# Two attentions of a hybrid mixer: matmul order, rotation, and where sigmoids and values stand

## The chip, the cores and the metric

The kernel runs on one core of a Trainium2 chip. The metric is the device time of one execution in microseconds (us), lower is better. In the profile, PE is the matrix engine (TensorE), PEld its weight loads, DVE the vector engine, ACT the scalar engine (activations, copies, casts), POOL is GpSimd, SP the engine whose queue issues the DMAs. SBUF is the core's working memory with 128 partitions, PSUM the eight accumulator banks that PE writes.

## The reference, cut to what matters

The program is three transformer layers on 512 tokens of 1024 features. The change touches the mixer of the first layer, which sees 16 extra tokens in front (528 in all). It has two attentions of eight heads over the same input:

```python
# first attention ("stick breaking"): q, k, v of 64 columns a head
z = (q @ k.T) * 64 ** -0.5
log_1m = where(strict, log_sigmoid(-z), 0); csum = cumsum(log_1m)
a = where(strict, exp(log_sigmoid(z) + csum[-1] - csum), 0);  y_sb = (a @ v) @ w_sb_o
# second attention ("latent"): q, k, v from normed latents c_q (384), c_kv (256)
s = (q_nope @ k_nope.T + rope(q_rope) @ rope(k_r).T) * 96 ** -0.5   # 64 + 32 columns a head
p = softmax(where(chunk mask, s, -1e30));                 y_mla = (p @ v) @ w_mla_o
# rope(x): x1, x2 = halves of 16 columns -> [x1*cos - x2*sin, x1*sin + x2*cos]; k_r is shared by all heads
g = sigmoid(gate_pre + b_gate)                                  # two gates of 1024 columns
out = (g_sb * y_sb + g_mla * y_mla) @ w_out
```

## The kernel before, in words

Activations lie transposed: 128 features on the partitions, tokens along the columns. Every projection is made in three passes for precision: weights and inputs are split into a rounded part and a remainder (hi, lo), and hi*hi, hi*lo and lo*hi are added in PSUM. A weight tile is loaded by a DMA on SP's queue (`wdma`, line 277), then cast by ACT (line 286) and its remainder made by DVE (line 287); two raw and three cast buffers are in turn. Attention scores, transposes and value products are in plain float32, and each of their matmuls is two PE instructions in the trace.

Instructions are written in program order, and a planner sorts each engine's queue: among instructions that it thinks ready it takes the one with the lowest place in program order. `high_priority(offset=n)` moves what is written under it n places ahead. On the chip each engine then runs its queue strictly in that order.

Both attentions go through four pairs of heads (c = 0 to 3), and in each through four blocks of 128 queries (b = 0 to 3), whose keys grow from 144 to 528. `start(c, b)` writes the scores (line 721, and the mask as a matmul, line 724) and the chain on ACT and DVE that makes probabilities of them. `attn_t` transposes the probabilities on PE (line 672; the 16 last keys in line 684) and copies them out of PSUM (line 677). `attn_v` multiplies them with the values (line 695). While a chain runs, PE is given filler: `self.todo` holds generators that write projection matmuls (`step_lin`, line 343), one matmul for each step, or two of half width where all 528 keys are projected, and `fill(n)` takes n steps. In the first attention the filler is the next pair's q and k and the 16 tiles of the gates, in the latent one the next pair's q and k and the eight tiles of y_sb @ w_sb_o (`wo`). The scores of block b + 1 are written before the transposes of block b. Transposes, value products and their copies are all under `high_priority(offset=100)`.

In the first attention the two heads of a pair lie on partitions 0 to 63 and 64 to 127, and their score matmuls use one half of PE's rows each. In the latent one each head has its own tiles of 96 rows: 64 rows without rotation, and 32 with it. The rotated queries are made from four weight tiles: for each group of four heads one with the rotated columns, one with the halves of these columns swapped. `turn` multiplies the first by the cosine and the second by the signed sine, and DVE adds the two into each head's q (in `qdone`). The rotated key rows `kr` are copied by ACT into each head's k, eight times. PSUM holds two double banks for scores (z), two banks for projections (l) and two for transposes and value products (a).

Before the latent attention all 16 tiles of the two gates (`gs`, `gm`) go through the sigmoid on ACT. Then come the first pair's projections, the latent values (line 910, five token blocks of six matmuls), and the loop over pairs. Its filler `wo` takes 2, 1, 2 and 3 tiles for the four pairs. After it the output stage makes y_mla @ w_mla_o (line 301), multiplies by gm, adds gs, splits the sum (lines 291, 292) and multiplies by w_out. ACT holds one set of function tables at a time: one for exponential and logarithm, one for the sigmoid, one for the square root.

## Time and profile before

| | us |
|---|---|
| median of 3 runs (2532.6 to 2533.84) | 2532.71 |
| the profiled execution | 2533.2 |
| its span | 2531.4 |
| PE busy over the span | 2496.9 (99%), 13334 matmuls |
| DVE busy | 1360.7 (54%) |
| ACT busy | 993.6 (39%) |
| first attention | about 481 to 681 |
| latent attention | about 681 to 797 |
| output stage up to w_out | about 797 to 815 |

Times in the rows count from the span's start. The span is what lies between the first and the last instruction of the profiled execution. A matmul's end is modelled, so two matmuls of the timeline overlap, and the distance from one start to the next tells what PE gave to each. An idle time in square brackets stands before the instruction, with the instruction that ended it.

### The profile page before, as it was taken

How to read it: one execution, taken by the hardware profiler on the slowest of the kernel's cores; microseconds unless marked ns; L12 is line 12 of the kernel's file. 1: busy time of each engine (PE TensorE's matmuls, PEld its weight loads, DVE VectorE, ACT ScalarE, POOL GpSimd, SP SyncE). 2: the span in 40 equal slices, each digit the busy share in tenths (PEclk: the TensorE clock that was granted, in tenths of full speed). 3: DMA queues.
4: the chain of work that ended last, by engine and by line, in shares of the span. 5: the costliest groups of instructions: out<-in, count | busy, mean ns of one | idle time of the engine just before them, and what ended most of it. 6: DMA issues, size and time to landing. Idle time of an engine off the chain costs nothing.

```text
span 2531.4 us, 33257 instructions
## 1 busy us (share of the span) xinstructions
PE 2496.9 (99%) x13334; PEld 2081.7 (82%) x13334; DVE 1360.7 (54%) x2197; ACT 993.6 (39%) x1601; POOL 162.3 (6%) x159
## 2 busy tenths in 40 slices
PE   8999999999999999999999999999999999999999
PEld 8999998777677788888777888888888668888887
DVE  5323347455566562434668765345465775535544
ACT  4222235344654442223564633223344563323332
POOL 1101010000001010101001011001000001101100
PEclk9999999999999999999999999999999999999999
DMA  4322234212212433333322332332333123333332
GB/s 140 92 92 85 92 95 132 81 54 67 59 43 64 161 116 92 97 100 98 115 89 90 118 107 91 93 109 92 93 114 101 42 76 133 94 98 100 96 89 100
DMA packets 78932, 240.49 MB, mean 95 GB/s; under 512 B 9332, under 2 KB 11636, under 8 KB 78520
## 3 DMA queue, kind: packets, MB, share of 16 engines
q1 hardware_dynamic: 78776, 238.35, 30.4%
q8 instruction: 105, 1.72, 0.3%
q14 instruction: 51, 0.42, 0.1%
HBM read 226.24 MB, written 8.92 MB: 93 GB/s over the span
## 4 chain that ended last, share of the span: by engine, by line
PE 91%; DVE 4%; ACT 3%; issue 1%; DMA 1%; POOL 0%; SPq 0%; ACTq 0%; DVEq 0%
PE l L301 71%; PE l L328 5%; PE l L343 5%; PE l L314 2%; PE z L721 1%; PE a L695 1%; PE a L672 1%; ACT e L236 1%; PE s L1414 1%; DVE wlo L287 1%; ACT whi L286 1%; PE a L408 1%; PE a L393 1%; DMA wraw<-in_hyo 1%; PE a L1442 1%
## 5 line engine op out<-in xcount | busy, mean ns | idle before, releaser
L286 ACT CAST whi<-wraw 128x1024 fp32r<-128x1024 f32 (+4 forms) x456 | 432.9, 950 | 1032.1 <-PE l L301 781.7
L301 PE MATMUL l<-xh,whi 128*128 128x512 f32 (+3 forms) x2156 | 707.9, 355 | 0.0
L301 PE MATMUL l<-xh,wlo 128*128 128x512 f32 (+3 forms) x2156 | 705.8, 354 | 0.0
L301 PE MATMUL l<-xl,whi 128*128 128x512 f32 (+3 forms) x2156 | 705.5, 354 | 0.0
L287 DVE TENSOR_TENSOR wlo<-wraw,whi 128x1024 fp32r<-128x1024 f32 (+4 forms) x456 | 500.2, 1098 | 274.9 <-ACT whi L286 268.8
L301 PEld LDWEIGHTS l<-xh,whi 128*128 128x128 f32 (+1 forms) x2156 | 382.1, 188 | 56.9 <-issue 1.4
L301 PEld LDWEIGHTS l<-xh,wlo 128*128 128x128 f32 (+1 forms) x2156 | 381.9, 188 | 56.6 <-issue 1.0
L301 PEld LDWEIGHTS l<-xl,whi 128*128 128x128 f32 (+1 forms) x2156 | 382.2, 187 | 56.2 <-issue 1.2
L301 PE MATMUL l<-chh,wlo 128*128 128x512 f32 x384 | 149.4, 389 | 0.0
L301 PE MATMUL l<-chl,whi 128*128 128x512 f32 x384 | 149.4, 389 | 0.0
L301 PE MATMUL l<-chh,whi 128*128 128x512 f32 x384 | 149.4, 389 | 0.0
L301 PE MATMUL l<-hh,wlo 128*128 128x256 f32 (+2 forms) x528 | 140.3, 320 | 0.0
L301 PE MATMUL l<-hl,whi 128*128 128x256 f32 (+2 forms) x528 | 140.2, 320 | 0.0
L301 PE MATMUL l<-hh,whi 128*128 128x256 f32 (+2 forms) x528 | 140.1, 319 | 0.0
L247 POOL TENSOR_TENSOR t<-g,xrs 128x528 f32<-128x528 f32 (+1 forms) x44 | 75.1, 1708 | 646.0 <-ACT g L236 646.0
L247 POOL TENSOR_TENSOR cc<-cc,xrs 128x512 f32<-128x512 f32 x48 | 62.8, 1308 | 834.1 <-ACT cc L236 830.3
L247 DVE TENSOR_TENSOR t<-l,t 128x256 f32<-128x256 f32 (+1 forms) x66 | 32.3, 516 | 143.9 <-PE l L301 138.9
L301 PEld LDWEIGHTS l<-hh,whi 128*128 128x128 f32 x528 | 88.4, 188 | 6.9
L301 PEld LDWEIGHTS l<-hl,whi 128*128 128x128 f32 x528 | 88.2, 188 | 6.9
L301 PEld LDWEIGHTS l<-hh,wlo 128*128 128x128 f32 x528 | 88.3, 188 | 6.8
L247 DVE TENSOR_TENSOR g<-l,xrs 128x256 f32<-128x256 f32 (+1 forms) x66 | 32.3, 516 | 114.3 <-PE l L301 112.6
L247 DVE TENSOR_TENSOR cz<-l,xrs 128x512 f32<-128x512 f32 x48 | 33.2, 692 | 109.6 <-PE l L301 105.3
(350 smaller groups left out, 3463.6 us busy)
## 6 DMA issues: line engine op xcount, KB each, us to landing
wraw<-in_up SPq DMA_DIRECT2D x96, 512.0 KB, 3.5
wraw<-in_dn SPq DMA_DIRECT2D x64, 384.0 KB, 3.2
wraw<-in_ffn_g SPq DMA_DIRECT2D x44, 512.0 KB, 3.5
wraw<-in_ffn_u SPq DMA_DIRECT2D x44, 512.0 KB, 3.4
wraw<-in_ffn_d SPq DMA_DIRECT2D x32, 448.0 KB, 3.3
wraw<-in_hy SPq DMA_DIRECT2D x20, 512.0 KB, 3.5
wraw<-in_ffn_d SPq DMA_DIRECT2D x16, 512.0 KB, 3.6
wraw<-in_gate SPq DMA_DIRECT2D x16, 512.0 KB, 3.5
```

What stands on the lines that cost most here:

```text
L236: i = nc.scalar.activation(out, in_, f, **kw)
L247: return (eng or self.nc.vector).tensor_tensor(out, a, b, op=op)
L286: nc.scalar.copy(hi, raw)
L287: nc.vector.tensor_tensor(lo, raw, hi, op=ALU.subtract)
L301: self.nc.tensor.matmul(ps, a[:, k * m:(k + 1) * m], b[:, k0 + k, c0:c1], start=first and k == 0 and pi == 0, stop=last and k == kc - 1 an ...
L314: self.nc.tensor.matmul(ps[:c1 - c0, :n], a[:, k, c0:c1], b[:, j * n:(j + 1) * n], start=k == 0 and pi == 0, stop=k == nk - 1 and pi == 2)
L328: self.nc.tensor.matmul(ps, a[:, k * P:(k + 1) * P], b[:, k0 + k, t0:t1], start=k == 0 and pi == 0, stop=k == kc - 1 and pi == 2)
L343: self.nc.tensor.matmul(ps, a[:, k * P:(k + 1) * P], b[:, k, t0:t1], start=k == 0 and pi == 0, stop=k == kc - 1 and pi == 2)
L393: nc.tensor.matmul(ps[:w, i * 64:(i + 1) * 64], acc[:, c:c + w], self.ones[:, :64], start=True, stop=True)
L408: nc.tensor.matmul(p[:, c - a:c - a + w], r[:w, i:i + 1].to_broadcast([w, P]), self.ident[:w, :w], start=True, stop=True)
L672: nc.tensor.transpose(pt[:, j * P:(j + 1) * P], probs[hh][:, i * P:(i + 1) * P], self.ident)
L695: nc.tensor.matmul(po[64 * hh:64 * hh + 64, :], vt[:, i, (2 * c + hh) * 64:(2 * c + hh + 1) * 64], where[(i, hh)], start=i == 0, stop=i == nb)
```

## The change

Six things are changed, all in the first layer's mixer.

- `step_lin` with two=True takes one PSUM bank, runs all matmuls of the first 256 keys, evicts them, and then does the same for the other 272. Before, both banks were taken and the matmuls of the two alternated.
- The matmuls of `attn_t`, `last_keys` and `attn_v` no longer stand under the raised priority; only the copies out of PSUM do.
- The latent rotation takes two weight tiles, one with the first halves of all eight heads' rotated columns and one with the second halves. `turn` makes both products of each with cosine and sine, then their difference and sum, once for all heads (`turned`). Two DMAs for each head's q bring its rows; q and k have 128 rows now, 64 of them for the rotation, of which k is zero in the rows that belong to the other head.
- The keys' rotated rows are brought once, by eight DMAs, into four lasting tiles (two for each head of a pair), whose upper halves POOL sets to zero first.
- The eight sigmoids of gs stand behind the first pair's latent projections; those of gm stand in the output stage, two tiles ahead of their use.
- The latent values are written behind the first scores in place of six filler steps. The first pair's copies of q and k go to DVE. `wo` takes two tiles for each pair, and the numbers of filler steps differ.

```diff
@@ prep, consts @@
-    r["uq"] = np.concatenate([_wt(nope), _wt(rope), _wt(_swap(rope, 16))], axis=0)
+    rope = rope.reshape(384, 8, 2, 16).transpose(0, 2, 1, 3).reshape(384, 256)
+    r["uq"] = np.concatenate([_wt(nope), _wt(rope)], axis=0)
...
+    r["rope8"] = np.ascontiguousarray(np.stack([np.tile(t[:, META:], (8, 1)) for t in (cos, sin)], axis=1).astype(np.float32))
@@ step_lin @@
-        segs, ev = self.banks2() if two else self.banks1(c0)
-        for k in range(kc):
-            for pi, (a, b) in enumerate(((hi, x[0]), (hi, x[1]), (lo, x[0]))):
-                for ps, t0, t1 in segs:
-                    self.nc.tensor.matmul(ps, a[:, k * P:(k + 1) * P], b[:, k, t0:t1],
...
-                yield
-        with self.tc.high_priority(offset=1000):
-            done(ev)
+        n = 0
+        for c0, c1 in ((0, CUT), (CUT, TM)) if two else ((c0, c0 + T),):
+            ps = self.bank()[:, :c1 - c0]
+            for k in range(kc):
+                for pi, (a, b) in enumerate(((hi, x[0]), (hi, x[1]), (lo, x[0]))):
+                    self.nc.tensor.matmul(ps, a[:, k * P:(k + 1) * P], b[:, k, c0:c1],
                                           start=k == 0 and pi == 0, stop=k == kc - 1 and pi == 2)
+                    n += 1
+                    if not two or n % 2 == 0:
+                        yield
+            with self.tc.high_priority(offset=1000):
+                done(ps, c0, c1)
@@ mixer @@
-        for g, b in ((gs, 0), (gm, KD)):
-            for m in range(KD):
-                self.act(g[:, m, :], g[:, m, :], AF.Sigmoid, bias=self.v("b_gate", b + m))
+        def sigmoid(g, m):
+            self.act(g[:, m, :], g[:, m, :], AF.Sigmoid, bias=self.v("b_gate", m + (KD if g is gm else 0)))
...
+        for m in range(2):
+            sigmoid(gm, m)
         for m in range(KD):
+            if m < KD - 2:
+                sigmoid(gm, m + 2)
             ps = self.lin1(d["wo"][m][:, 512:], ymla, 4)
@@ attn_t (attn_v and last_keys alike) @@
-        with self.tc.high_priority(offset=100):
-            for g0 in range(0, len(slots), 4):
...
+        for g0 in range(0, len(slots), 4):
...
+            with self.tc.high_priority(offset=100):
                 (nc.vector.tensor_copy if (g0 // 4) % 2 else nc.scalar.copy)(at[:, :n1], pt[:, :n1])
@@ latent @@
+        ks = [[L.tile([P, TM], F32, name=f"k{hh}{i}") for i in range(2)] for hh in range(2)]
+        for i in range(2):
+            for hh in range(2):
+                k = ks[hh][i]
+                nc.gpsimd.memset(k[64:, :], 0.0)
+                for s_ in range(2):
+                    p = 64 + 32 * s_ + 16 * hh
+                    nc.sync.dma_start(k[p:p + 16, :], kr[16 * s_:16 * s_ + 16, :])
+        turned = L.tile([P, 2, T], F32, name="turned")
...
+                    def done(ps, a, b):
+                        self.tt(turned[:, j, :], ps, rope[:, 0, :], mul)
+                        self.tt(t[:, 1 - j, :], ps, rope[:, 1, :], mul)
+                        if j:
+                            self.tt(turned[:, 0, :], turned[:, 0, :], t[:, 0, :], ALU.subtract)
+                            self.tt(turned[:, 1, :], turned[:, 1, :], t[:, 1, :], add)
...
-                    q = L.tile([96, T], F32, name=f"q{hh}", bufs=2)
-                    self.copy(q[:64], ev[0][0][64 * hh:64 * hh + 64])
-                    i = 2 * (c % 2) + hh
-                    self.tt(q[64:96], t12[32 * i:32 * i + 32, 0, :], t12[32 * i:32 * i + 32, 1, :], add)
+            copy = nc.vector.tensor_copy if c == 0 else self.copy
+                    q = L.tile([P, T], F32, name=f"q{hh}", bufs=2)
+                    copy(q[:64], ps[64 * hh:64 * hh + 64])
+                    for s_ in range(2):
+                        nc.sync.dma_start(q[64 + 32 * s_:96 + 32 * s_, :], turned[32 * c:32 * c + 32, s_, :])
...
-                    for p, s in ev:
-                        self.copy(s(k[:64]), p[64 * hh:64 * hh + 64])
-                    self.copy(k[64:96], kr)
+                    copy(ks[hh][c % 2][:64, a:b], ps[64 * hh:64 * hh + 64])
...
+        sigmoids()
         for c in range(4):
-            nm = (2, 1, 2, 3)[c]
+            nm = 2
...
-            self.fill(6)
+            if c == 0:
+                values()
+            else:
+                self.fill(4)
             for b in range(4):
                 if b < 3:
                     nxt = start(c, b + 1)
-                    self.fill(5)
+                    self.fill(5 if b else 4)
                 t = self.attn_t(L, probs, c, b + 1, vt, ymla, b, rest[b % 2])
-                self.fill(4)
+                self.fill((3, 4, 4, 3)[b])
                 if b < 3:
                     self.attn_v(*t)
-                    self.fill(3 if b == 2 else 1)
+                    self.fill(5 if b == 2 else 1)
```

## Rows read from the trace of the kernel before

**Rows 1.** Table of stretches: engine, busy us (instructions); PEclk granted clock; DMA share, GB/s.
```profile
481.00:681.00 200.00, 193.68 (x1119) 144.38 (x1118) 112.16 (x179) 91.02 (x163) 3.39 (x31) 1.00 0.19 59
681.00:700.00 19.00, 16.39 (x76) 12.33 (x76) 8.23 (x15) 16.98 (x32) 0.00 (x0) 1.00 0.29 84
700.00:797.00 97.00, 94.87 (x641) 70.56 (x641) 64.04 (x176) 51.37 (x138) 0.00 (x0) 1.00 0.14 42
797.00:815.00 18.00, 18.00 (x79) 14.59 (x79) 8.83 (x15) 5.62 (x10) 8.34 (x5) 1.00 0.30 87
```

**Rows 2.** Timeline, PE: start us, us, engine, line, operation, out<-in, shapes [idle before <-releaser].
```profile
681.75 0.40 PE L343 MATMUL l<-cqh,whi 128*128 128x512 f32 x1
...
687.66 0.39 PE L343 MATMUL l<-cqh,wlo 128*128 128x512 f32 x1
```

**Rows 3.** Timeline, head of the latent attention, DVE, ACT and PE.
```profile
684.65 0.69 DVE L247 TENSOR_TENSOR t<-l,rope 128x512 f32<-128x512 f32 x1
...
684.85 3.18 ACT L236 ACTIVATE gm<-gm,vecs 128x512 f32<-128x512 f32 x5
...
689.90 1.18 ACT L243 COPY q<-l 64x512 f32<-64x512 f32 x2
...
691.13 0.40 PE L343 MATMUL l<-ckvh,whi 128*128 128x272 f32 x1 [2.37 <-ACT q L243]
...
699.70 0.65 PE L721 MATMUL z<-k,q 96*128 96x144 f32 x4
```

**Rows 4.** Table of PE's waits, first attention: us in total, times, longest.
```profile
PE a L672 <- ACT e L236: 3.9, 9, 0.7
PE l L343 <- DVE sbk L247: 2.1, 4, 0.6
```

**Rows 5.** Table of PE's waits, latent attention.
```profile
PE l L343 <- ACT q L243: 3.1, 2, 2.4
```

**Rows 6.** Chain of work that ended last, first attention: start us, us, what.
```profile
507.33 0.87 PE z L721 x2
...
520.26 0.64 PE z L721 x2
...
521.49 0.65 PE z L721 x4
...
561.04 0.64 PE z L721 x2
```

**Rows 7.** Timeline, PE, behind a value product of the latent attention.
```profile
743.14 0.50 PE L343 MATMUL l<-ysbl,whi 128*128 128x512 f32 x1
743.48 0.40 PE L343 MATMUL l<-ysbh,wlo 128*128 128x512 f32 x1
```

**Rows 8.** Timeline, PE, last transposes of the latent attention.
```profile
791.13 0.44 PE L672 MATMUL a<-cst,e 128*128 128x128 f32 x2 [1.09 <-DVE e L894]
```

**Rows 9.** Timeline, ACT, table load behind the first attention's last exponential.
```profile
673.64 1.28 ACT L232 ACT_TABLE_LOAD   x1
...
674.93 0.59 ACT L677 COPY at<-a 128x512 f32<-128x512 f32 x1
```

**Rows 10.** DMA issues: count, KB each, median us from issue to landing.
```profile
qt<-ra SPq DMA_DIRECT2D x32, 64.0 KB, 2.0
```

**Rows 11.** Timeline, PE, latent scores and transposes.
```profile
712.70 1.50 PE L721 MATMUL z<-k,q 96*128 96x264 f32 x6
714.04 0.71 PE L672 MATMUL a<-cst,e 128*128 128x128 f32 x5
714.58 0.38 PE L684 MATMUL a<-cst,e 128*16 128x128 f32 x2
```

**Rows 12.** Timeline, PE, last block of the second head pair, latent attention.
```profile
740.78 0.22 PE L724 MATMUL z<-masks,idb 128*128 128x128 bf16 x1
...
745.55 0.27 PE L672 MATMUL a<-cst,e 128*128 128x128 f32 x1
```

More of the change, by code (lines that the diff above doesn't have):

```diff
@@ L638, in mixer @@
             if True:
-                self.latent(st, cq, ckv, kr, masks[:, P:], ymla, ysb, gs)
+                self.latent(st, cq, ckv, kr, masks[:, P:], ymla, ysb, gs, lambda: [sigmoid(gs, m) for m in range(KD)])
         stP.close()
@@ L823, in stick, with latent @@
         self.attn_v(*late)
-    def latent(self, st, cq, ckv, kr, mask, ymla, ysb, gs):
+    def latent(self, st, cq, ckv, kr, mask, ymla, ysb, gs, sigmoids):
         nc, d = self.nc, self.d
@@ L828, in latent @@
         L = self.pool(st, "L")
-        rope = L.tile([P, 2, TM], F32, name="rope")
-        nc.sync.dma_start(rope, d["rope"])
+        rope = L.tile([P, 2, T], F32, name="rope")
+        nc.sync.dma_start(rope, d["rope8"])
         scale = float(96 ** -0.5)
@@ L834, in latent @@
         nc.gpsimd.memset(vt[:, 4, :], 0.0)
-        t12 = L.tile([P, 2, T], F32, name="t12")
+        ks = [[L.tile([P, TM], F32, name=f"k{hh}{i}") for i in range(2)] for hh in range(2)]
+        for i in range(2):
+            for hh in range(2):
+                k = ks[hh][i]
[4 more added lines that the diff above has]
+        turned = L.tile([P, 2, T], F32, name="turned")
@@ L836, in latent, with turn, done @@
         qk = {}
         def proj(c):
-            def turn(j):
-                def done(ev):
-                    self.tt(t12[:, j, :], ev[0][0], rope[:, j, META:], mul)
-                return done
-            if c % 2 == 0:
+            if c == 0:
+                t = L.tile([P, 2, T], F32, name="t12")
+                def turn(j):
+                    def done(ps, a, b):
+                        self.tt(turned[:, j, :], ps, rope[:, 0, :], mul)
[3 more added lines that the diff above has]
+                            self.tt(turned[:, 1, :], turned[:, 1, :], t[:, 1, :], add)
+                    return done
@@ L866, in wo, with done @@
         def wo(m):
-            def done(ev):
-                self.tt(gs[:, m, :], ev[0][0], gs[:, m, :], mul)
+            def done(ps, a, b):
+                self.tt(gs[:, m, :], ps, gs[:, m, :], mul)
             yield from self.step_lin(d["wo"][m][:, :512], ysb, 4, done)
@@ L903, in latent, with values @@
         self.fill()
-        w = self.wload(d["uv"][0], 1024)
-        for i in range(5):
-            a, b = i * P, min((i + 1) * P, TM)
-            ps = self.bank()[:b - a]
-            for k in range(2):
-                for pi, (xx, ww) in enumerate(((0, 0), (1, 0), (0, 1))):
-                    nc.tensor.matmul(ps, ckv[xx][:, k, a:b], w[ww][:, k * 512:(k + 1) * 512],
-                                     start=k == 0 and pi == 0, stop=k == 1 and pi == 2)
-            self.copy(vt[:b - a, i, :], ps)
+        def values():
+            w = self.wload(d["uv"][0], 1024)
+            for i in range(5):
+                a, b = i * P, min((i + 1) * P, TM)
+                ps = self.bank()[:b - a]
+                for k in range(2):
+                    for pi, (xx, ww) in enumerate(((0, 0), (1, 0), (0, 1))):
+                        nc.tensor.matmul(ps, ckv[xx][:, k, a:b], w[ww][:, k * 512:(k + 1) * 512],
+                                         start=k == 0 and pi == 0, stop=k == 1 and pi == 2)
+                self.copy(vt[:b - a, i, :], ps)
+        sigmoids()
         late, m = None, 0
         for c in range(4):
-            nm = (2, 1, 2, 3)[c]
+            nm = 2
             self.todo = ([proj(c + 1)] if c < 3 else []) + [wo(m + i) for i in range(nm)]
```

63 lines of the change are left out of this document (30 added, 33 removed).

## The prediction

> **What bounds the kernel now.** I read the page's busy shares first: TensorE (PE) is busy almost all the time, no other engine much above half. Then the table of stretches: the granted clock is 1.00 in all of them, PE stays 2 to 6 us short of full in each stretch of the attentions, and VectorE (DVE) and ScalarE (ACT) are busy for about half of each, DVE for two thirds in the latent one [rows 1]. Only at the head of the latent attention does ACT lead, with 16.98 of 19.00 us. So the time is the sum of what PE executes, of what it loses in changing between kinds of matmul, and of its waits. A step of the change is worth what it takes from that sum; work that leaves ACT or DVE counts only through a wait of PE, for which I read the table of waits and then the timeline around each. The profiled execution took 2533.2 us, its span is 2531.4, the median of the runs 2532.71; the sum below is made on the first, and 0.5 us comes off for the median.
>
> **The parts and their costs.**
>
> *Two projection tiles fewer.* The rotated queries took four weight tiles (plain and swapped columns, for two groups of heads), now two. A tile is 3 slices by 3 passes, so 18 matmuls go. 26 intervals of these matmuls take 687.66 - 681.75 = 5.91 us, 0.227 each [rows 2]: 4.1 us. Bounds 0 (where they stood, in the middle of the stage, they covered a softmax) and -4.1; I take -4.1, since PE was nearly full there. Two weight loads with their casts go too, off the path: 0.
>
> *Head of the latent attention.* From 681.75 to 699.70, 17.95 us, PE executes 27 matmuls at 0.227 (6.1), 12 of about half width at 0.12 (1.5) and the values' 30 at 0.23 (6.9): 14.5, so 3.4 us are lost. Most of it is 2.37 us in which the second half of the key projection waits for a copy on ACT, which stands behind gm's sigmoids at 0.64 us each [rows 3]. The change takes those eight sigmoids away, puts the copies of the first head pair on DVE, and emits the values behind the first scores, where they cover the softmax. What is late next is DVE: after the second rotated tile it has four multiplies or adds at 0.69 [rows 3], as the product with rope there, 2.8 us, and six copies out of PSUM, by the same row at most 4.1, while PE needs 3.5 us for the query and key projections left. With two banks the second key piece still waits for the query's. I leave 1.5 us of wait: -1.9; bounds 0 and -3.4.
>
> *Projections over all keys, one half after the other.* Both banks were taken at once and came free together. PE waited for that four times, 2.1 us, in the first attention [rows 4], and 3.1 - 2.37 = 0.7 us in the latent one beside the wait already counted [rows 5]. Now one half is evicted while the other's matmuls run. Of 2.8 us I take -2.5; bounds 0 and -2.8.
>
> *Transposes at their written place.* The priority let them jump up to 100 places, ahead of filling matmuls, as soon as the planner thought the exponentials done. On the chip they were not: PE waits 3.9 us for ACT in nine places of the first attention [rows 4]. Behind the 14 to 22 filling matmuls (3.2 to 5 us) that now stay in front they are. I take -3.5; bounds 0 and -3.9.
>
> *Scores of two heads side by side.* The first attention's score matmuls use 64 rows each. In the last block those of one head (x2) take 0.64 us of the chain, those of two heads together (x4) 0.65 [rows 6]. The pair forms only where nothing of full height stands between. In the last block of queries the priority puts transposes and value products there: the x2 at 561.04 is the first of four that stand alone in one block [rows 6]. Over the four head pairs 12 of 16 run alone and 4 in two pairs, 14 x 0.64; in written order it is 8 x 0.64: -3.8. The third block's eight, 0.87 each (at 507.33 in [rows 6]), could save 3.5 more, but there the second head needs the PSUM tile that the block before it has just used, and I count 0. Bounds 0 and -7.3.
>
> *Fewer broken value products.* A visit to the 64-column value products lengthens the matmul after it to 0.34 us (743.48 - 743.14) from 0.23 [rows 7]; I take the same for the one before it, 0.2 a visit. Ten of the 32 visits of both attentions are split into two or three. Joining half of them: -1.0; bounds 0 and -2.0. In return a product now stands at a fixed 1 to 6 matmuls behind its transposes, while the copy between them needs 0.6 us and two hand-overs, about 1.1. Where the planner fills with other work it costs nothing; I add +3.0, 0.2 us for each of 16 latent blocks, bounds 0 and +6.4 (0.4 each).
>
> *Tail of the latent attention.* The last head pair has two output tiles to fill with, not three: 12 matmuls, 2.8 us. Even with three, PE waits 1.09 us for the last softmax [rows 8]. The next stage's matmuls can stand in. +1.0; bounds 0 and +2.8.
>
> *Sigmoids of gm in the output stage.* ACT was busy 5.62 of 18 us there [rows 1]. Eight at 0.64 and one more table load of 1.28, right behind which ACT goes on [rows 9], make it 12.0, and one tile comes every 12 x 0.227 = 2.7 us. Cost 0; bounds 0 and +1.3 (cover gone: the load in front of the last transposes' copy).
> The Trainium skill speaks against this step: ScalarE: Activation LUTs, section "What ACT_TABLE_LOAD costs", counts a drain of 1.38 us beside the load, 2.66 in all. In this trace the copy behind the load starts 0.01 us after it [rows 9], so the drain is not seen. By the page the sum would be at worst 2.7 us longer, by the row 1.3.
>
> *DMAs instead of copies and adds.* Sixteen transfers bring the rotated rows to the queries and eight fill the keys' rows once; eight ACT copies and eight DVE adds go. A 64 KB transfer inside the core lands after 2.0 us [rows 10]. On SP's queue the later ones are issued a head pair ahead of their use, and the weight loads behind them keep three tiles of lead; only the first scores come soon after, with the values' 6.9 us to stand in. 0; bounds 0 and +2.0. Scores now span 128 rows, not 96. A 96-row score takes 1.34 / 6 = 0.22 us for 264 columns, a 128-row transpose 0.54 / 5 = 0.11 for 128 [rows 11], the same per column: 0.
>
> Sum: -4.1 - 1.9 - 2.5 - 3.5 - 3.8 - 1.0 + 3.0 + 1.0 = -12.8. 2533.2 becomes 2520.4, by the runs' median 2519.9; the forecast is 2520.
>
> **The rivals.**
>
> *More of it, 2511.* No new waits at the value products (-3.0), the third block's scores side by side as well (-3.5), the head's wait gone (-1.5) and the other splits too (-1.0): -21.8. For it: the waits in the rows are of the planner's making. Against: its guesses about the other engines were wrong before and may be so again.
>
> *Given back, 2529.* Priorities only shift which wait is paid, and the planner still takes what it thinks ready. The matmuls (-4.1) and half of the gains at the two-bank waits (-1.0) stay, the tail's +1.0 comes on top: about -4. For it: PE is busy for 97% of both attentions [rows 1]. Against: four terms rest on instructions or banks, not on the order.
>
> *Slower, 2543: the softmax shows.* The latent attention covers each softmax by a fixed number of fillers. For the last block these are 5 + 4 + 5 matmuls, the third block's 16 transposes and its value products, 3.2 + 1.7 + 1.2 = 6.1 us; the chain itself took 4.7, from the last score's mask at 740.78 to the transpose at 745.55 [rows 12]. If DVE's added copies and ACT's casts stretch it so that each of the 16 blocks waits 1.5 us, 24 us come on top of -12.8: +11.2, less 0.5 for the median. It decides from 12.8 / 16 = 0.8 us a block. Against it: 1.4 us of slack in the longest chain, and a planner that takes other work.
>
> **How the numbers follow.** I call 0.2% (5.1 us) the least that is told from no change. Forecast 0.58, more of it 0.18, given back 0.15, slower 0.09. Given back lies near the edge: 0.02 of it faster, 0.12 the same, 0.01 slower. So faster 0.78, same 0.12, slower 0.10. All gains at their ends without a new cost, -23.5, give 2509; the terms are rough, and the range 2507 to 2532 goes 2 us past that and on the other side up to the time of before, which leaves out the slower case. The likeliest case's own range is 2514 to 2526.
>
> **What would show it.** Right: 18 fewer matmuls on the query latents; score matmuls x4 in the last block of queries; no wait of PE for the first attention's keys; waits for exponentials under 1 us there; the values behind the first scores, and under 2 us of waits before these. Wrong: as many scores alone as before, new waits for the transposes' copies or for the rotated rows' DMA, or PE busy for less than 97% between the first latent scores and the output stage.

## The result, and the profile after

The changed kernel takes 2509.97 us (median of 4 runs, 2507.91 to 2512.61); the kernel before, on the same chip, 2533.28 (4 runs, 2532.6 to 2534.64). The ratio is 0.9908, 95% interval 0.9891 to 0.9925: 23.3 us faster. The forecast was 2520. That is inside the stated range and outside the likeliest case's own one (2514 to 2526); the time lies at the rival "more of it", 2511, though only in part by that rival's terms (below). The profiled execution of the changed kernel took 2507.91 us, its span is 2506.1.

Where the time went is read from the starts of first matmuls in PE's timeline. The table gives the distances between these landmarks: the first matmul of the mixer (the projection that makes the latents), the first score of the first attention, the first matmul that reads the query latents (head of the latent attention), the first matmul of w_out on the mixer's sum, and the first one of the second layer's part behind it.

| us | before | after | difference |
|---|---|---|---|
| span's start to the mixer's first matmul | 450.70 | 447.86 | -2.8 |
| first projections, up to the first score | 44.64 | 43.87 | -0.8 |
| first attention | 186.42 | 170.61 | -15.8 |
| latent attention and output stage up to w_out | 133.82 | 130.21 | -3.6 |
| w_out and what follows, up to the second layer | 467.06 | 464.47 | -2.6 |
| the rest | 1248.78 | 1249.12 | +0.3 |

The first line lies ahead of everything that the change touches. Over the 14 profiled executions it varies from 446.8 to 450.7 us with the same 3492 matmuls in the same order. Most of that is one step: from the 200th to the 2900th of these matmuls four executions take 330.56 us (before, runs 1, 3 and 7) and ten take 328.57, with the clock granted at 1.00 in all. The two kernels that were profiled twice agree with themselves (447.86 and 447.60, 447.76 and 448.00), so it may belong to the kernel and not to the execution; it is no part of the change's mechanism, and its cause stays open. Some 2 us of a difference between a kernel of one group and one of the other can come from there; the other lines of the table are free of it.

The table of stretches of the changed kernel, with the columns of [rows 1]: most of the first attention, the head of the latent attention, its body, the output stage.

```profile
462.00:662.00 200.00, 199.48 (x1188) 155.10 (x1188) 112.69 (x182) 96.86 (x169) 2.99 (x30) 1.00 0.20 64
662.00:675.40 13.40, 9.69 (x51) 7.37 (x48) 8.93 (x18) 3.00 (x6) 2.53 (x5) 1.00 0.41 119
675.40:775.00 99.60, 97.03 (x654) 72.34 (x654) 61.39 (x173) 54.79 (x145) 0.02 (x1) 1.00 0.18 53
775.00:792.00 17.00, 17.00 (x77) 14.08 (x76) 12.54 (x17) 9.21 (x15) 7.07 (x5) 1.00 0.37 108
```

In the first attention PE is busy for 199.48 of 200 us, where it was 193.68 [rows 1]. The head of the latent attention got worse: 9.69 of 13.40 us, 72%, after 16.39 of 19.00, 86%. ACT is nearly free there now (3.00 us, it was 16.98), and PE still loses 3.7 us.

The table of PE's waits of the changed kernel, first attention (total, times, longest), the counterpart of [rows 4]:

```profile
PE a L704 <- ACT at L686: 0.4, 2, 0.2
```

And its latent attention, the counterpart of [rows 5]:

```profile
PE l L346 <- DVE t L249: 2.5, 1, 2.5
PE a L680 <- DVE e L917: 1.2, 2, 0.7
PE l L346 <- DVE q L878: 0.9, 1, 0.9
PE a L704 <- ACT at L686: 0.4, 2, 0.2
PE a L704 <- DVE at L686: 0.4, 1, 0.4
PE l L934 <- DVE wlo L289: 0.3, 1, 0.3
PE l L346 <- ACT q L245: 0.2, 1, 0.2
```

Of 6.0 us of waits for exponentials and key tiles in the first attention nothing is left, and 0.4 us for the copies of transposes is all that is new. The latent attention's waits did not shrink: they sum to 5.9 us, and 4.4 were there before (3.1 of [rows 5], 1.1 of [rows 8] and 0.2).

The chain of work that ended last in the changed kernel, third and last block of queries of the first head pair (start us, us, what), the counterpart of [rows 6]:

```profile
503.25 0.88 PE z L731 x4
504.13 0.22 PE z L734 x2
504.35 4.31 PE l L346 x22
508.66 0.44 PE a L680 x4
...
512.64 1.09 PE z L731 x8
513.73 0.22 PE z L734 x2
```

Four scores of the third block, both heads, take 0.88 us; two of one head took 0.87 before [rows 6]. All eight scores of the last block stand together and take 1.09 us.

In the other three head pairs the last block takes 1.09, 1.09 and 1.16 us, but the third block's four take 1.16, 1.16 and 1.58: by PE's timeline the second head's first score starts 0.3 to 0.7 us behind the first head's there.

### The profile page after: what moved, and what is told of

It is laid out like the page before. It is cut to its first block, busy times and chain, and to the rows that moved or that the text cites. A ratio compares the mean times of both kernels' runs of the same rounds, so it can differ in the third digit from the quotient of the medians.

```text
span 2506.1 us, 33264 instructions
## 1 busy us (share of the span) xinstructions
PE 2477.9 (99%) x13316; PEld 2074.8 (83%) x13316; DVE 1358.0 (54%) x2195; ACT 986.8 (39%) x1586; POOL 163.4 (7%) x163
## 4 chain that ended last, share of the span: by engine, by line
PE 94%; DVE 3%; ACT 1%; issue 1%; DMA 1%; POOL 0%; SPq 0%; ACTq 0%; DVEq 0%
PE l L303 73%; PE l L346 6%; PE l L330 5%; PE l L316 2%; PE z L731 1%; PE a L704 1%; PE s L1443 1%; DVE wlo L289 1%; PE a L413 1%; PE a L680 1%; PE a L398 1%; PE a L1471 1%; PE a L1465 0%; ACT e L238 0%; DVE h L249 0%
```

## The experiments

All are timed in five rounds beside the kernel before, with a 95% interval of the ratio. "First attention" and "latent" are the third and the fourth line of the table above, taken in the same way.

**1. The order alone.** The kernel before, with nothing of the change but the lifted priority:

```diff
-        with self.tc.high_priority(offset=100):
-            for g0 in range(0, len(slots), 4):
-                ...
+        for g0 in range(0, len(slots), 4):
+            ...
+            with self.tc.high_priority(offset=100):
+                (nc.vector.tensor_copy if (g0 // 4) % 2 else nc.scalar.copy)(at[:, :n1], pt[:, :n1])
```

> The kernel before with one edit: the matmuls of transposes and value products leave the raised priority, in both attentions. If the order carries most of the gain (theory), the first attention, 186.4 us before, falls by 12 to 14 us: 7.3 for the scores of two heads side by side in the last two blocks, 5 to 6 for waits for exponentials; the median is then about 2520. If the priority only shifts which wait is paid (rival), and the halves of the key projection and the smaller rotation carry the gain, it stays above 2528. In the latent attention I expect nothing from it, -2 to +2.

Measured: 2517.08 us (2515.59 to 2518.24), ratio 0.9937 [0.9925, 0.9949]. The first attention takes 171.26 us, 15.2 less than before; the latent stretch 132.52. So the order gives 16 of the 23 us, nearly all of it in the first attention. It also does most of what I had booked under the key projections in halves. This is the table of PE's waits in this kernel, which still takes both banks at once, from the mixer's first projections to the end of the first attention:

```profile
PE l L343 <- DVE sbk L247: 0.5, 1, 0.5
```

That wait was 2.1 us in four places [rows 4]. The one that is left stands at 492.18, in the first projections; in the first attention itself nothing is left.

**2. The priority back.** The changed kernel with that one edit undone:

> The changed kernel with the matmuls of transposes and value products under the raised priority again. Theory: about 4 us come back for scores that stand alone again (the plan has the heads apart in the third block of three head pairs and in half of the last block of two), and 5 to 6 for waits for exponentials, so the median is near 2520, 10 above the changed kernel. Rival (the order is worth little): 2510 to 2513.

Measured: 2531.75 us (2528.77 to 2533.58), ratio 0.9994 [0.9985, 1.0003], no different from before. Undoing the order in the changed kernel costs 21.7 us, more than it gives in the kernel before and twice what I expected: 10.8 in the first attention (181.40 us) and 9.8 in the latent one (140.05; runs 8 and 10 take that apart). The other parts together are worth next to nothing under the old priority.

**3. Scores of the two heads apart.** The changed kernel; in the last two blocks of the first attention each head's scores are followed by its mask at once, a full-height matmul between the heads:

```diff
-        for row in zip(*todo):
...
+        if apart and len(units) == 2:
+            rows = [[r] for r in todo]
+        else:
+            rows = [todo]
+        for todo in rows:
+            for row in zip(*todo):
...
```

> The changed kernel with the first attention's scores of the last two blocks written head by head, each with its mask (a matmul of full height) right behind, so that no two heads' scores stand next to each other; the number of instructions is the same. Theory: the pairs are worth 3.8 us in the last block and 3.5 in the third, so the median is 7 us above the changed kernel, near 2517, and the score matmuls of 264 columns show 0.64 us alone. Rival (another wait takes the place, the pairs were worth under 2 us): 2510 to 2512.

Measured: 2517.67 us (2515.55 to 2519.73), ratio 0.9939 [0.9925, 0.9952]: 7.6 us slower than the changed kernel. The chain of work that ended last in this kernel, the same two blocks as above:

```profile
504.94 0.86 PE z L736 x2
505.81 0.16 PE z L739
505.97 0.87 PE z L736 x2
506.83 0.16 PE z L739
...
515.29 1.08 PE z L736 x4
516.38 0.16 PE z L739
516.54 1.08 PE z L736 x4
517.62 0.16 PE z L739
```

Four scores of one head take 1.08 us, eight of two heads 1.09: standing together, the second head's cost nothing. The first attention takes 178.83 us, 8.2 more.

**4. The changed kernel again,** on the chip of runs 1 to 3:

> The changed kernel once more, as a control: 2510 us. Its profile was 2.8 us shorter than that of before in the 450 us ahead of the mixer, where the matmuls stand in the same order. If that was the one execution, it is gone here; if it is of the kernel, the first matmul of the latent projections' stage (line 316, first start 447.9 us) stands again 2 to 3 us earlier than the 450.7 of before.

Measured: 2510.10 us (2509.49 to 2513.78), ratio 0.9912 [0.9899, 0.9926]. The mixer's first matmul stands at 447.60, again 3 us earlier than before: by what I had written down, that is of the kernel and not of one execution.

**5. Both banks at once.** The changed kernel with the old projection:

```diff
-        for c0, c1 in ((0, CUT), (CUT, TM)) if two else ((c0, c0 + T),):
-            ps = self.bank()[:, :c1 - c0]
+        cuts = ((0, CUT), (CUT, TM)) if two else ((c0, c0 + T),)
+        segs = [(self.bank()[:, :b - a], a, b) for a, b in cuts]
...
```

> The changed kernel (2510.0 us), but a projection of the keys takes its two PSUM banks at once again and alternates between them, as before. Theory: the halves are worth what the waits of line 343 for keys' tiles were worth while the rest of the order was already the new one: about 2 us in the first attention at most and about 0.5 in the latent one, so 2511 to 2513; the stretch from the first scores to the first cq product goes from 170.6 to 171 to 173. Rival one (the prediction's step): 2.5 to 2.8 us, 2512.5 to 2513, with waits of TensorE for DVE's keys back in the rows. Rival two: the halves are worth nothing once scores stand in pairs (the evictions have time), 2509.5 to 2510.5. Rival three, the other side: whole halves cost weight loads that two banks share, so that going back is a gain, 2507 to 2509.

Measured: 2511.13 us (2510.6 to 2511.45), ratio 0.9913 [0.9899, 0.9926]; 1.1 us by the medians, less than the runs can tell from nothing. The landmarks are finer: first projections 44.65 us (+0.8, of which 0.5 is a wait for a key tile), first attention 171.33 (+0.7, where PE waits for no key tile at all). The latent stretch is 130.79 (+0.6 and +1.1 against the two executions of the changed kernel), but its granted clock is 0.57 from 670.5 to 674.5, behind the wait for the rotation's table (run 6): that costs 1.7 us, which neither of the two executions has, and it is more than the difference. So the halves show 1.5 us in two places, and nothing in the latent attention.

**6. The rotation's table early.** The changed kernel, with a place of its own for the table and its load ahead of the first attention:

```diff
+            self.rope8 = self.pool(stG, "R", side=self.other).tile([P, 2, T], F32, name="rope8")
+            nc.sync.dma_start(self.rope8, d["rope8"])
             if True:
                 self.stick(S, x, n.rs, vt, ysb, masks[:, :P], gs, gm)
...
-        rope = L.tile([P, 2, T], F32, name="rope")
-        nc.sync.dma_start(rope, d["rope8"])
+        rope = self.rope8
```

> The changed kernel, but the table of the latent rotation has a place of its own and is loaded ahead of the first attention, not into memory that this attention gives back. Theory: TensorE's wait of 2.5 us at the first latent head comes from this transfer (issued at 662.8, landed at 667.8); without it the rotation's two products start at the eviction, and 1.5 to 2.5 us go: 2507.5 to 2508.5; the stretch from the first cq product to the first latent scores goes from 12.8 or 13.1 to 10.5 to 11.5. Rival: DVE's four products and two sums of the rotation, and the DMAs of the turned rows behind them, are as late without it, and 0 to 0.7 us go: 2509.3 to 2510.0, the stretch stays above 12.3.

Measured: 2506.77 us (2505.15 to 2510.98), ratio 0.9898 [0.9885, 0.9912]; the stretch from the first matmul on the query latents to the first latent score goes from 13.06 to 9.81 us, the latent one from 130.21 to 127.41. Timeline of the changed kernel, head of the latent attention (start us, us, engine, line, operation, names, shapes, idle before):

```profile
661.80 0.55 DVE L289 TENSOR_TENSOR wlo<-wraw,whi 128x384 fp32r<-128x384 f32 x1
...
662.33 0.50 PE L346 MATMUL l<-cqh,whi 128*128 128x512 f32 x1
662.38 0.33 SPq L279 DMA_DIRECT2D wraw<-in_uv  x1
662.47 0.53 POOL L843 MEMSET mlav<- 128x512 f32 x1 [1.57 <-PE a L704]
662.80 0.38 SPq L839 DMA_DIRECT2D rope<-in_rope  x1
...
667.80 0.69 DVE L249 TENSOR_TENSOR turned<-l,rope 128x512 f32<-128x512 f32 x1 [2.44 <-DMA rope<-in_rope]
669.23 0.47 PE L346 MATMUL l<-cqh,whi 128*128 128x512 f32 x1 [2.51 <-DVE t L249]
```

The same DVE instruction with the table there in time, 2.4 us after that kernel's first matmul on the query latents at 662.22:

```profile
664.61 0.69 DVE L249 TENSOR_TENSOR turned<-l,rope 128x512 f32<-128x512 f32 x1
```

This settles which transfer the head waits for. The wait is put down to DVE in the table of waits, but DVE itself waited 2.44 us for a transfer of 512 KB that was issued at 662.80, half a microsecond behind the head's first matmul. In the kernel before it was issued at 678.54, 3.2 us ahead of the head at 681.75 [rows 2], and nothing waited for it. Run 1, the old kernel in the new order, has the wait as well: 1.51 us of DVE for the table.

Why it is issued so late has two reasons in the trace, and the runs don't separate them. The tile lies in memory that the first attention gives back, and in written order that attention's last value products stand directly in front of the head; POOL's write into the latent values' tile, of the same pool, waits for them until 662.47. In the kernel before, the priority had pulled them forward. But the load of the values' weights (in_uv) also stands in front of the table on SyncE's queue now, which it did not before, and it waits for a raw buffer until DVE is done with it at 662.35. Run 6 takes the table out of both.

**7. All sigmoids ahead of the latent attention,** as before; the rest as changed:

```diff
+                for g in (gs, gm):
+                    for m in range(KD):
+                        sigmoid(g, m)
-                self.latent(st, cq, ckv, kr, masks[:, P:], ymla, ysb, gs, lambda: [sigmoid(gs, m) for m in range(KD)])
+                self.latent(st, cq, ckv, kr, masks[:, P:], ymla, ysb, gs, lambda: None)
...
-        for m in range(2):
-            sigmoid(gm, m)
         for m in range(KD):
-            if m < KD - 2:
-                sigmoid(gm, m + 2)
```

> The changed kernel, but all 16 sigmoids stand ahead of the latent attention again, and none in the output stage. Theory: ScalarE needs about 16 times 0.6 us there while the first copies of q and k are on VectorE, so little waits: 0 to 1 us slower, 2509.5 to 2511. Rival: the first latent softmaxes and copies of values stand behind the sigmoids on ScalarE, and 2 to 5 us are lost between the first cq product and the output stage: 2512 to 2515.

Measured: 2512.45 us (2511.63 to 2517.05), ratio 0.9924 [0.9911, 0.9936]: 2.4 us slower by the medians, at the rival's edge and above my theory. But that is not shown to be the edit's. The stretch ahead of the mixer is 450.43 us here, 2.6 to 2.8 longer than in the changed kernel. The head costs 14.68 us in place of 13.06, and the table of stretches shows why, a lower granted clock (0.83 over 10 us costs 1.7) behind the wait for the table, a wait which the changed kernel has as well:

```profile
670.00:680.00 10.00, 6.93 (x27) 5.45 (x28) 7.80 (x13) 2.45 (x5) 0.00 (x0) 0.83 0.25 61
```

PE's waits in the latent attention sum to 5.3 us, not more than the 5.9 and 5.6 of the changed kernel. At w_out PE waits 1.5 us for the remainder of its weights on DVE, as it did before (817.82, 1.50 us behind DVE's wlo) and as it doesn't in the changed kernel; but runs 2, 8, 9 and 11 have that wait too (0.9 to 1.5 us), with the sigmoids where the changed kernel has them.

**8. The priority back in the latent attention alone:**

```diff
+        with self.tc.high_priority(offset=100) if self.ahead else ExitStack():
             for g0 in range(0, len(slots), 4):
                 ...
```

> The changed kernel, but in the latent attention alone the transposes, value products and their matmuls take their priority back; the first attention stays as changed. Theory: the two losses of the run with the priority back in both attentions (10.8 us in the first, 9.5 in the latent) are separate, so this kernel loses the second alone: 2518 to 2520, with the first attention at 170.6 and the latent stretch from the first cq product to the output at 126 to 128 (118 as changed). Rival: the latent loss was a consequence of the state that the first attention left (tiles and engines late), so here 0 to 4 us: 2510 to 2514.

Measured: 2515.69 us (2514.13 to 2520.98), ratio 0.9935 [0.9921, 0.9949]: 5.6 us slower, between theory and rival. The latent stretch is 134.03 us, 3.8 more than changed and 6.0 less than in run 2. One wait and what follows it make that up, the last transposes for the last exponential in PE's timeline:

```profile
770.28 0.41 PE L681 MATMUL a<-cst,e 128*128 128x128 f32 x2 [3.39 <-ACT e L238]
```

In written order matmuls of the output stage stand in that place (the waits there are 0.51 and 0.73 us). That is 2.1 us; behind the wait the granted clock falls (0.66 from 770 to 775), which costs 1.7 more. Run 2 has the same 3.39 us at 786.20, and the same fall behind it (0.57 from 786 to 790); where its other 6 us come from, run 10 shows.

**9. The values ahead of the first latent scores,** with the old split of output products over the pairs and the old counts between steps:

```diff
+        values()
         sigmoids()
...
-            nm = 2
+            nm = (2, 1, 2, 3)[c]
...
-            if c == 0:
-                values()
-            else:
-                self.fill(4)
+            self.fill(6)
...
```

> The changed kernel, but the values' products stand ahead of the first latent scores again, with the old split of the output's products over the pairs and the old counts between steps. Theory: behind the first scores the values cover the first softmax, which otherwise nothing but six steps of other projections covers; the place and the counts are worth 1 to 3 us: 2511 to 2513, with the stretch from the first cq product to the output stage 130.9 to 133 (129.7 and 130.2 as changed). Rival: under the written order nothing waits for the first softmax either way, since the next pair's projections stand there, so 0 within 0.7 us: 2509.5 to 2510.8; the whole latent gain is then the 18 matmuls.

Measured: 2510.64 us (2508.04 to 2512.3), ratio 0.9912 [0.9898, 0.9925]. The rival holds for the time: by the medians the values' place and the counts are worth nothing. The latent stretch is 127.43 us, 2.8 shorter, and w_out's stretch is 467.47, 3.0 longer. There PE waits 0.9 us for w_out's weights; 1.7 us are a fall of the clock (0.66 from 838 to 843), which one of the two executions of the changed kernel has in that place too.

**10. The rotation alone.** The kernel before with the rotation by whole halves and the keys' rotated rows made once. The first pair's copies of q and k also go to DVE here, as in the changed kernel; nothing else of the change is in it:

> The kernel before (2533) with the latent rotation and the keys' rotated rows of the changed one, and nothing else of it: priority, both banks at once, sigmoids and values as before. Theory: two projection tiles fewer, 18 matmuls at 0.23 us, give 4.1 us, and the wait for the table's transfer at the head, 2.2 to 2.5 us as in the changed kernel, replaces the wait of 1.9 that was there: 2528.5 to 2530, first attention as before (186). If that comes, the loss of 9.8 us that the run with the priority back showed in the latent attention belongs to the values' place under the priority, not to the rotation. Rival: the rotation by DMAs (two for each query tile) is what loses under the priority, since the first scores wait for the turned rows: 2533 to 2540, with waits of the scores for those DMAs.

Measured: 2537.34 us (2531.98 to 2540.27), ratio 1.0017 [1.0008, 1.0025]: slower than before, by 4.3 us, although PE executes 18 matmuls fewer. The latent stretch is 137.14 us, 3.3 longer. PE's timeline at the first latent scores of this kernel:

```profile
689.41 1.04 PE L728 MATMUL z<-k,q 128*128 128x144 f32 x4 [0.25 <-DMA q<-turned]
690.84 0.48 PE L728 MATMUL z<-k,q 128*128 128x144 f32 x2 [0.39 <-DMA q<-turned]
...
693.12 0.94 PE L728 MATMUL z<-k,q 128*128 128x400 f32 x2 [1.06 <-ACT e L238]
...
697.21 1.96 PE L728 MATMUL z<-k,q 128*128 128x264 f32 x4 [1.93 <-ACT e L238]
...
699.04 0.77 PE L931 MATMUL l<-whi,ckvh 128*128 128x512 f32 x1
```

My theory falls. The rival has the time right, but not the wait: the scores themselves wait only 0.6 us for the DMAs of turned rows. But the values, which in the program stand in front of these scores, come at 699.04, behind the scores of three blocks of queries and of one head of the fourth. SyncE's queue in the timeline of this kernel points to the reason:

```profile
677.88 4.38 SPq L850 DMA_DIRECT2D k<-kr  x7
686.75 4.95 SPq L877 DMA_DIRECT2D q<-turned  x8
691.74 0.59 SPq L850 DMA_DIRECT2D k<-kr  x1
692.42 0.53 SPq L279 DMA_DIRECT2D wraw<-in_uv  x1
```

The load of the values' weights (in_uv) stands behind the sixteen new transfers in the queue: 0.62 us to issue each, and the queue waits 4.4 us for DVE's turned rows besides. In the kernel before it was issued at 683.14, 1.4 us behind the head's first matmul, here at 692.42, 12.5 us behind it. What PE finds in its place are the scores of later blocks, each of which needs a PSUM tile that the exponentials of an earlier block give back: 3.0 us of waits with nothing in between. The table of stretches of this kernel, over the scores and right behind:

```profile
689.40:699.00 9.60, 6.22 (x27) 3.86 (x28) 6.67 (x21) 4.79 (x15) 0.00 (x0) 0.92 0.39 116
699.00:705.00 6.00, 6.00 (x29) 4.36 (x29) 2.89 (x9) 2.60 (x7) 0.00 (x0) 0.85 0.24 66
```

PE is busy for 65% of the first stretch, and the granted clock falls in both. In the whole latent attention PE's waits sum to 7.4 us, 3.0 more than before, and the fall of the clock costs 1.7. So the 18 matmuls fewer, 4.1 us, are paid back there with more. w_out's stretch is 2.3 us longer as well; its waits are not, but the clock falls twice in it (0.57 from 820 to 824 and from 868 to 872), behind waits that the kernel before has without a fall. So a part of the 4.3 us is the clock's.

Run 2 shows the same: in_uv issued at 685.46, behind its sixteen transfers, and the same two waits for ACT (1.05 and 1.93 us), with the clock at 0.66 from 690 to 695. Of the 9.8 us of its latent stretch 3.2 are waits (all of them together, 9.1 against 5.9), 3.4 two falls of the clock, and the other 3.3 are spent without either, with value products in 31 visits in place of 18. In the changed kernel, and in run 9, in_uv is issued ahead of the table and of all these transfers (662.38 and 662.80 in the changed one). That the late load is the cause, and that the planner found its buffer free in time with the written order, is read from the traces; a kernel with that one load moved was not tried.

**11. One output product more in the last pair of latent heads,** on top of run 6:

```diff
-            nm = 2
+            nm = (1, 2, 2, 3)[c]
```

> The version with the rotation's table loaded early (2506.8), with one of the output's products moved from the first pair of latent heads to the last (1, 2, 2, 3 in place of 2 each). Theory: at the end of the latent attention, where the last pair's softmaxes find little behind them (waits for DVE's e of 1.2 us and for the copies), one more product of 12 matmuls, 2.8 us of work, covers them: 0.5 to 1.5 us faster, 2505.3 to 2506.3. Rival: the first pair then lacks cover for its own softmaxes and the wait only moves: 2506.3 to 2508.5.

Measured: 2506.33 us (2504.8 to 2508.82), ratio 0.9897 [0.9883, 0.991]. The latent stretch falls as the theory says, to 125.26 us, 2.1 less than in run 12. But w_out's stretch grows by 5.0, to 469.43. PE's timeline there:

```profile
786.48 0.50 PE L330 MATMUL l<-ooh,whi 128*128 128x512 f32 x1
786.81 0.40 PE L330 MATMUL l<-ool,whi 128*128 128x512 f32 x1
788.71 0.50 PE L330 MATMUL l<-ooh,wlo 128*128 128x512 f32 x1 [1.50 <-DVE wlo L289]
...
790.02 0.63 PE L330 MATMUL l<-ooh,whi 128*128 128x512 f32 x1
790.44 0.63 PE L330 MATMUL l<-ool,whi 128*128 128x512 f32 x1
```

PE comes to w_out before DVE has made the remainder of its weights. It waits 1.50 us, and then seven matmuls start 0.43 us apart and not 0.23, while the table of stretches of that kernel shows the clock near its lower level:

```profile
790.00:793.00 3.00, 3.00 (x9) 2.36 (x8) 2.92 (x5) 0.62 (x1) 0.00 (x0) 0.52 0.77 221
793.00:800.00 7.00, 7.00 (x33) 5.79 (x32) 3.77 (x6) 2.81 (x4) 0.00 (x0) 1.00 0.87 299
```

A second fall, behind the wait for DVE's acc (0.57 from 837 to 841), makes up the rest of the 5.0; runs 6 and 12 have that wait without it.

**12. Run 6 again,** beside run 11:

> The version with the rotation's table loaded early once more, beside the run that moves a product, on the same chip: 2505.5 to 2508 (2506.8 the first time); a ratio to the kernel before of 0.9885 to 0.9912 again. If it lies above 2509, the gain of 3.3 us over the changed kernel was the chip's.

Measured: 2506.31 us (2506.02 to 2507.59), ratio 0.9897 [0.9882, 0.9912]. Run 6's version is 3.2 to 3.8 us below the changed kernel by the medians, on two chips. The intervals of the two ratios overlap; that this is a gain rests on the landmarks, where the latent stretch is 2.3 to 2.8 us shorter in both executions, with the clock at 1.00 in these and in the changed kernel's. It is the best version found; run 11 doesn't differ from it.

## Why the prediction was right, and where its terms were not

The direction, the place of the largest gains and the mechanism held: the time is the sum of what PE executes and its waits, and the priority was paying for nothing. The sum was -12.8 and the median moved by 23.3. Of the signs that I had named for being right one failed: PE waits 3.7 us before the first latent scores, not under 2. That the time came out at the rival "more of it" is luck in part: the third block's scores and the missing new waits came, mostly, but that rival also has the head's wait gone, which grew, and in its place stand the 2.8 us ahead of the mixer. By its own steps:

*Scores of two heads side by side, -3.8: the term that was mis-sized most.* Counting the distances from a group of scores to the next matmul over the first attention, all scores take 22.83 us before and 13.67 after, -9.2. But 1.9 of it are the waits of the next step: in the second block the scores stood directly in front of transposes that waited for their exponentials, as here in PE's timeline of the kernel before, and the distance takes the wait in.

```profile
540.95 0.73 PE L721 MATMUL z<-sbk,sbq 64*128 64x272 f32 x4
...
542.10 0.44 PE L672 MATMUL a<-cst,e 128*128 128x128 f32 x2 [0.42 <-ACT e L236]
```

That leaves -7.3, the far end of the step's bounds. The last block gives 4.6, from 12 groups alone at 0.64 and 2 pairs at 0.65 to four groups of eight at 1.09 to 1.16. The third block gives 2.5, 7.3 to 4.8 us; I had counted it at 0, because its second head needs the PSUM tile of the block before. In written order that tile comes early enough for the first head pair (0.88 us), in part for the next two (1.16) and hardly for the last (1.58). The second block gives 0.3. Run 3 shows the mechanism: apart, the scores take 20.08 us, the first attention 8.2 more. The Trainium skill states it in TensorE: Matmul & The Clock Gate, section "Why this matters for your kernels": matmuls with fewer than 128 rows run concurrently where each has its own group of rows. Here 1.08 us for four alone and 1.09 for eight agree.

*Transposes at their written place, -3.5: right.* The 3.9 us of [rows 4] are gone, and run 1 shows that the order takes them.

*Projections in halves, -2.5: near in sum, wrong in its parts.* The order alone takes 1.6 of the 2.1 us (run 1). The halves are worth 0.8 in the first projections, where one of the four waits stood, and 0.7 in the first attention without any wait there to explain it (run 5). In the latent attention nothing is shown.

*Two projection tiles fewer, -4.1: the matmuls go, their price alone is not shown.* Those on the query latents go from 72 to 54. The latent stretch loses 3.6 to 4.1 us, with 1.1 to 1.5 us more of waits in it.

*DMAs instead of copies and adds, 0 within 0 to +2.0: right for this kernel, and only by its company.* I argued that the weight loads behind the new transfers keep three tiles of lead. In the kernel before they don't: there the rotation, with its 18 matmuls fewer, costs 4.3 us in all, with the values' weights late and the clock lower behind the waits (run 10). With the written order that load goes ahead of the transfers. The rival "given back" expected such an exchange of one wait for another, but from the order and not from the rotation.

*Head of the latent attention, -1.9: wrong, +1.1.* By PE's busy time the head lost 2.6 us of 19.00 before [rows 1] and loses 3.7 of 13.40 now. I named DVE as next late. It is, by 0.9 us (the copies of q; 1.2 in run 6); but ahead of it stands the table's DMA, which I had costed at 0 within 0 to +2.0, on the transfers of rotated rows. I followed the transfers that the change adds, and not the one whose issue time the new order moves: it delays the table, by its memory, by what stands in front of it on the queue, or by both, and the wait is 2.5 us (run 6).

*New waits at the value products, +3.0: mis-sized.* They are 1.2 us in both attentions together (the three rows of L704 above); the planner filled the rest, as the rival had it. *Fewer broken value products, -1.0:* visits to them go from 42 to 34 in both attentions, 8 at 0.2 us a visit, -1.6 worked out; not tested by itself.

*Tail, +1.0:* the last waits for exponentials sum to 1.2 us, 1.1 before [rows 8], so nothing was lost there. A third output tile takes 2.1 us from the stretch (run 11), but w_out takes it back.

*Sigmoids of gm in the output stage, 0: no cost is seen, and no gain is shown.* The table load there is 1.28 us and nothing of PE waits for it. The 2.4 us of run 7 are no more than what the stretch ahead of the mixer differs by. The wait of 1.5 us for w_out's weights is gone in the changed kernel, but other kernels with the sigmoids in this place have it.

*The rival "slower"* should read 2544 by its own sum (2533.2 + 11.2 - 0.5), and the chain in [rows 12] is 4.8 us, so that its slack is 1.3; neither changes the argument. It asked for 0.8 us of uncovered softmax in each of the 16 latent blocks. In the changed kernel the waits for exponentials sum to 1.2 us; where cover did go, in runs 2 and 10, it was for one head pair, 3.0 us.

The errors in one line: -3.5 at the scores, -1.8 at the value products, -1.0 at the tail, -0.6 each at the split visits and the halves, -0.4 at the transposes, against +3.0 at the head. That is -4.9 of the -10.5 us between the sum and the medians' difference. Another 2.8 lie ahead of the mixer, and 1.5 are the wait at w_out; the last 1.3 I can't assign.

## What to carry to other kernels

A priority that lets instructions jump the written order is worth what the planner's picture of the other engines is worth: look in the trace whether the jumping instructions then wait, and whether they stand between matmuls that would run side by side. When an order changes, follow each transfer whose issue it moves, by the memory it waits for and by what stands in front of it on its queue, not only the transfers that the change adds. An added transfer also costs what stands behind it: with sixteen small ones on the queue a weight load came late, and a change that removes matmuls was slower (run 10), until another edit let that load pass. And before a difference of 2 us between two traces is put down to an edit, compare the granted clock and a stretch that the edit doesn't touch.

## What the runs showed of the hardware

The granted clock was 1.00 throughout the mixer and behind it, from 481 to 870 us, in the profiled executions of the kernel before and of the changed one, and in runs 6 and 12. In the others it fell there to its lower level (1.2 GHz) for a few microseconds, each time behind a wait of PE, but not behind each wait:

| wait of PE | the clock falls behind it | it stays at 1.00 |
|---|---|---|
| for the table, 2.2 to 2.6 us | runs 3, 5, 7 | changed kernel (twice), runs 8, 9 |
| first latent scores for an exponential, 1.9 us | runs 2, 10 | |
| last transposes for an exponential, 3.4 us | runs 2, 8 | |
| for w_out's weights, 1.4 to 1.5 us | runs 10, 11 | before, runs 1, 2, 7, 8 |
| for DVE's acc in w_out's stretch, 2.0 us | changed kernel again (run 4), runs 1, 2, 3, 5, 7, 8, 9, 10, 11 | before, changed kernel, runs 6, 12 |

In run 11 matmuls of 0.23 us take 0.43 behind the wait of 1.50 us: about 1.7 us lost, more than the wait itself. The other falls cost the same; this is the one of run 4 in the table of stretches:

```profile
838.00:841.00 3.00, 2.69 (x11) 2.53 (x12) 0.34 (x2) 0.26 (x1) 0.00 (x0) 0.58 0.57 175
841.00:843.00 2.00, 2.00 (x13) 1.82 (x12) 0.33 (x1) 0.58 (x1) 0.00 (x0) 0.78 0.23 86
```

So a wait of PE here can have a price beside its length, and two executions of one kernel differ by it.

SyncE gave 0.62 us to each small transfer that it issued (eight of the turned rows in 4.95 us, seven of the keys' rows in 4.38), whether 33 or 64 KB, and 0.33 to the weight load in_uv (662.38).
